# Bulk loads issued by ScalarE on a queue of their own, and bias loads two rounds later, in a two-layer attention and retention trunk

## The chip, the cores and the metric

The kernel runs on one core of a Trainium2 chip. The metric is the device time of one execution in microseconds (us); the median of several runs counts. TensorE (PE) multiplies matrices, VectorE (DVE), ScalarE (ACT) and GpSimd (POOL) do the element-wise work, and SyncE (SP) does no arithmetic: in the kernel before it issues every DMA. The DMAs move data on 16 DMA engines.

## The reference

A trunk of two layers works on 2048 tokens of width 1024. Each layer does

```python
hn = rms_norm(x, norm_gain)
proj = hn @ w_in                      # 1024 -> 8 sections of 512
aq, ak, av, ag, rq, rk, rv, rg = split(proj)
ya = chunked_rel_attention(aq, ak, av, rel_bias)   # 8 heads x 64, own chunk of 64 + 8 before, bias by distance
yr = chunkwise_retention(rq, rk, rv, cos, sin)     # 4 heads x 128, decay per head, rotary phases, RMS norm per head
y = concat([ya * silu(ag), yr * silu(rg)])
x = x + y @ w_out
```

and a last RMS norm with a gain follows. All is float32; the kernel makes each product of a high and a low float16 part, in three matmuls.

## The kernel before, in words

**Tiling and stages.** A layer `l` is worked through in four groups `s` (two attention heads and one retention head each), and a group in four blocks `n` of 512 tokens. For each block `dense_T` makes q, k and the rotary inputs (lines 736 and before) and `dense_V` makes v and the gates (line 755); the attention and the retention of a block run beside the dense products of the next one. After the four groups `wout` multiplies by `w_out` (line 1105) and adds the residual, 16 blocks of 128 tokens.

**Rounds.** All is laid out by hand in rounds: `run` steps the dense generator (8 matmuls of 128x512 a step), then the attention, and then pulls some steps of the background list `bg`. `later(k, fn)` runs `fn` k rounds on. A block is 24 rounds. What the rounds call is recorded on PE, ACT, DVE and POOL in exactly that order:

```python
ctx.enter_context(tc.manual_schedule(engines={E.PE, E.Activation, E.DVE, E.Pool}))
```

SP is in that list only for the start of the program (`sp_order`, up to the end of the first `dense_V`). After that the order of what SP issues is made by the scheduler of the layer below, which may put a load ahead of its place in the source; only the `toep` DMAs are held at their place (`keep_in_program_order`).

**The background work.** `prep_T` and `prep_V` bring a group's weights (tiles `stT`, `stV`, 512 KB each, through `load_sec`), take the sum of their squares on ACT (`sumsq`, line 312), derive a power-of-two scale, and split them on ACT (line 333) and DVE (line 336). `prep_Omax` goes through the eight column blocks of `w_out` (tiles `stO0m` in layer 0, `stO1m` in layer 1): it squares one, then loads the next. `prep_O` loads and splits `w_out` itself (`stO`). They share a pool of three buffers (`w4`).

**Attention.** For each unit (128 queries of one head): scores on PE (lines 803 and 804), bias and maximum on DVE (807), exponential and float16 rounding on ACT (810, 812), the low part on POOL (813), one DMA transpose `pT<-pq` issued by SP (815), and the product with v on PE (823 to 825), which comes two units later.

**Other loads.** `bias_scratch` writes two Toeplitz tables `toep` in DRAM for a group (line 567), and `bias_tiles` reads a `bias` tile from each (580) and scales it on ACT (584). `tab_load` brings the rotary tables `tabc` and `tabs` of a block (623, 624). `y_load` (935) and `x_load` (944) bring the blocks that `wout` works on, `Sections` brings the small mask `msk` (359), `norms_from_input` the tokens of the first layer. SP also issues what the chains wait for: `pT<-pq`, the rearranged `q<-qq` and `k<-kk`, `swp`, `kt<-rot`, the stores to `y_d` and `x_d`, and the transposes of `wout` and of the norms.

**Semaphores of the DMAs.** The layer below deals eight semaphores in turn to all DMAs, whichever engine issues them, and a DMA waits until the one that had its semaphore before has landed.

Of the kernel before, what the change touches and what calls it, by code (L numbers as in the profile page):

```python
# [18 lines left out]
P = 128  # L19
EPS = 1e-6  # L20
HALF_PI = 1.5707963267948966
RELW = 767
# [5 lines left out]
def hybrid_trunk(ctx: ExitStack, tc: tile.TileContext, x, pos, gain, gcol, w_in, w_out, rel, fgain,  # L28
# [8 lines left out]
    act, dve, pool, pe, sp = nc.scalar, nc.vector, nc.gpsimd, nc.tensor, nc.sync  # L37
# [30 lines left out]
    y_d = [dp.tile([P, D], F32, tag=f"y_d{t}", name=f"y_d{t}") for t in range(NT)]  # L68
    x_d = [dp.tile([P, D], F32, tag=f"x_d{t}", name=f"x_d{t}") for t in range(NT)]
    tab_d = [dp.tile([2, P, 512], F32, tag=f"tab{n}", name=f"tab{n}") for n in range(NS)]  # L70
# [218 lines left out]
    TSEC = (0, 1, 4, 5)  # L289
    VSEC = (2, 6, 3, 7)  # L290

    def load_sec(src, nm, halves=False):

        v = src.rearrange("(k p) c -> p k c", p=P)
        if not halves:
            st = w4.tile([P, KT, P], F32, tag="w4", name=f"st{nm}")
            sp.dma_start(st, v)
            return [(st, 0, KT)]
        h = KT // 2
        st = [b2.tile([P, 3 - i, 512], F16, tag=("rot2", "rot3")[i], name=f"st{nm}_{i}") for i in range(2)]  # L300
        st = [t_[:, 0:2].rearrange("p a c -> p (a c)").bitcast(F32).rearrange("p (k c) -> p k c", c=P) for t_ in st]
        for i in range(2):
            sp.dma_start(st[i], v[:, i * h:(i + 1) * h, :])
        return [(st[i], i * h, (i + 1) * h) for i in range(2)]

    keep = lambda i: i
# [10 lines left out]
    def lowp(m1, nm):  # L317
        mb = b2.tile([P, 1], BF16, tag="mb", name=f"mb{nm}", bufs=4)
        dve.tensor_copy(mb, m1)
        return mb  # L320
# [33 lines left out]
    class Sections:  # L354


        def __init__(self, l, s, g, halves=False):
            g.msk = b2.tile([P, P], F32, tag="msk", name=f"msk{l}_{s}")
            sp.dma_start(g.msk, dmask[:, s, :])
            g.rd, g.s = rdc[:, s:s + 1], s  # L360
            self.l, self.s, self.g, self.halves = l, s, g, halves
            self.nm = f"T{l}_{s}"
            self.sts, self.sq, self.iv, self.sv = [], [None] * 4, [None] * 4, [None] * 4
            g.h = b3.tile([P, 4, KT, P], F16, tag="wh", name=f"wh{self.nm}")
            g.l = b3.tile([P, 4, KT, P], F16, tag="wl", name=f"wl{self.nm}")
# [102 lines left out]
    def prep_V_next(l, g):  # L468

        nm = f"V{l}_0"  # L470
        src = [w_in[l, :, VSEC[j] * 512:VSEC[j] * 512 + P] for j in range(4)]
        sts = [load_sec(src[j], f"{nm}{j}", True) for j in range(2)]
        yield
        for j in (2, 3):
            st = b2.tile([P, KT, P], F32, tag="q", name=f"st{nm}{j}")
            sp.dma_start(st, src[j].rearrange("(k p) c -> p k c", p=P))
            sts.append([(st, 0, KT)])
        yield
        g.vh = b3.tile([P, KT, 512], F16, tag="wh", name=f"wh{nm}")
        g.vl = b3.tile([P, KT, 512], F16, tag="wl", name=f"wl{nm}")  # L480
        hi, lo = ([w_[:, :, j * P:(j + 1) * P] for j in range(4)] for w_ in (g.vh, g.vl))
        m = [lowp(sumsq(sts[j], f"{nm}{j}", hi[j]), f"{nm}{j}") for j in range(2)]
        yield
        m2, m3 = (sumsq(sts[j], f"{nm}{j}", hi[j]) for j in (2, 3))
        dve.tensor_tensor(m2, m2, m3, op=ALU.add)
        m.append(lowp(m2, f"{nm}2"))
        yield
        yield
        iv = [None] * 3
        for j in (2, 0, 1):  # L490
            sv, iv[j] = norm_scale(allsum(m[j], f"{nm}{j}"), f"{nm}{j}", gains[l].i)
            for i in ((2, 3) if j == 2 else (j,)):
                yield from convert(sts[i], hi[i], lo[i], sv)
        yield from V_units(l, 0, g, iv, nm)
        g.vdone = 4
# [37 lines left out]
    toep = {}  # L533
    NH = 4 * 2 * DEPTH
    rel_d = dp.tile([NH, RELW + 1], F32, tag="rel_d", name="rel_d")
# [27 lines left out]
    def bias_scratch(l, s):  # L563
        for hh in range(2):
            h = 2 * s + hh
            d = dp.tile([P * RELW], F32, tag=f"toep{h % 4}", name=f"toep{l}_{h}")
            i = sp.dma_start(d.rearrange("(p w) -> p w", w=RELW),
                             rel_d[l * 8 + h:l * 8 + h + 1, 1:RELW + 1].to_broadcast([P, RELW]))
            if (l, s) != (0, 0):
                tc.keep_in_program_order(i)  # L570
            toep[l, h] = d
        yield

    def bias_tiles(l, s, g):

        g.bias = []
        for hh in range(2):
            h = 2 * s + hh
            bt = b3.tile([P, 640], F32, tag="bias", name=f"bias{l}_{h}")
            sp.dma_start(bt, toep[l, h][127:127 + P * (RELW - 1)].rearrange("(p w) -> p w", w=RELW - 1)[:, 0:640])  # L580
            yield
            pool.memset(bt[64:128, 0:64], NEG)
            pool.memset(bt[0:64, 576:640], NEG)
            act.activation(bt, bt, AF.Copy, scale=g.ci[:, 0:1])
            g.bias.append(bt)
            yield
# [28 lines left out]
    def dense_T(l, s, n, g, st):  # L615
# [4 lines left out]
        def tab_load():  # L620
            while n not in tab_done:
                pull(1)
            sp.dma_start(st.tabc, tab_d[n][0])
            sp.dma_start(st.tabs, tab_d[n][1])

        first = (l, s, n) == (0, 0, 0)

# [299 lines left out]
    def y_load(l, t):  # L927
        u = St()
        u.nm = f"y{l}_{t}"
        u.t = t  # L930
        if t < 8:
            u.y = w4.tile([P, D], F32, tag="w4", name=f"yy{u.nm}")
        else:
            u.y = b2.tile([P, D], F32, tag="q", name=f"yy{u.nm}")
        sp.dma_start(u.y, y_d[t])
        return u

    def x_load(l, u):
        if l + 1 == DEPTH or u.t < 12:
            f = (hT[l, 0] if l + 1 == DEPTH else hT_of(l + 1, NS - 1))[u.t // 2 % 2].rearrange("p k c -> p (k c)").bitcast(F32)  # L940
            u.x = f[:, u.t % 2 * D:(u.t % 2 + 1) * D]
        else:
            u.x = w4.tile([P, D], F32, tag="w4", name=f"xx{u.nm}")
        sp.dma_start(u.x, x[u.t * P:(u.t + 1) * P, :] if l == 0 else x_d[u.t])

    def y_squares(l, u):
        u.m = b2.tile([P, 1], F32, tag="ym", name=f"ym{u.nm}")
# [218 lines left out]
    def norms_from_input(ts, spaces, rows, tab):  # L1166

        def load(k):
            u = us[k]
            u.x = spaces[k] if spaces else w4.tile([P, D], F32, tag="w4", name=f"xin{u.t}")  # L1170
            if not spaces:
                sp.dma_start(u.x, x[u.t * P:(u.t + 1) * P, :])

        def sq(k):
            u = us[k]
            u.h = [h_[:, :, u.t % 4 * P:(u.t % 4 + 1) * P] for h_ in hT_of(0, u.t // 4)]
            u.ss = squares(u.x.rearrange("p (k c) -> p k c", c=P), u.nm, u.h[0])

        def root(k):
            us[k].rs = rms_of(us[k].ss, gains[0].m, gains[0].e, us[k].nm)  # L1180

        def mul(k):
            u = us[k]
            dve.scalar_tensor_tensor(out=u.x, in0=u.x, scalar=u.rs[:, 0:1], in1=gains[0].b, op0=ALU.mult, op1=ALU.mult)

        def hi(k):
            us[k].rows = rows[k % 2]
            rows_hi(us[k].rows, us[k].x)

        def lo(k):  # L1190
            rows_lo(us[k].rows, us[k].x)

        def dma(k):
            transpose_rows(us[k].rows, *us[k].h)

        us = []
        for t in ts:
            u = St()
            u.t, u.nm = t, f"n0_{t}"
            us.append(u)  # L1200
        plan = {0: [lambda: load(0)]}
        add = lambda r, fn, k: plan.setdefault(r, []).append(lambda: fn(k))
        for k in range(4):
            if k:
                add(4 * k - 4, load, k)
            for i, fn in enumerate((sq, root, mul, hi, lo, dma)):
                add(3 + 4 * k + i, fn, k)
        for r in range(21):
            for fn in plan.get(r, ()):
                fn()  # L1210
            next(tab, None)
            yield
        for _ in tab:
            yield
# [156 lines left out]
    for l in range(DEPTH):  # L1371
        gO = [Grp(), Grp()]
        go = Grp()
        for s in range(NSW):
            g = grp(l, s)
            for n in range(NS):
                first = (l, s, n) == (0, 0, 0)
                if not first:
                    st = St()
                    states[l, s, n] = st  # L1380
                    dT = dense_T(l, s, n, g, st)
                else:
                    st = st0
                if n == 0 and not first:
                    bs, bt = bias_scratch(l, s), bias_tiles(l, s, g)
                    later(1, lambda bs=bs: next(bs))
                    for k in (4, 8, 17, 21):
                        later(k, lambda bt=bt: next(bt))
                if (l, s) == (0, 0) and 0 < n < NS - 1:
                    if n == 1:  # L1390
# [30 lines left out]
                run(dense_V(l, s, n, g, st), att, 24 if n == NS - 1 and s < NSW - 1 else 12)  # L1421
                if first:
                    sp_order.__exit__(None, None, None)
                if att[0] is not None:
                    drain(att[0])
                att = [attention(l, s, n, g, st, states.get((l, s, n - 1)))]
# [84 lines left out]
```

## Time and profile before

| | |
|---|---|
| time, median of 3 runs | 2089.06 us (2085.99 to 2094.31) |
| time of the profiled execution | 2090.77 us |
| span of the profiled execution, first to last instruction | 2089.0 us |
| PE busy | 2007.5 us, 96% |
| ACT, DVE, POOL busy | 1145.0, 1177.1, 676.1 us (55%, 56%, 32%) |
| DMA queue | one (hardware_dynamic), 311.12 MB, 65.2% of 16 engines' span |
| mean granted TensorE clock | 0.992 |

"Busy" counts the instructions of an engine that compute; issues of DMAs are shown on the queue of the issuing engine (SPq for SP's) and are not counted as busy. "DMA to landing" is the time from the start of an issue until the semaphore shows that all of it has arrived. A line number is that of the kernel before. In the waits, "A <- B" says that A's engine stood idle until B was done.

### The profile page before, as it was taken

How to read it: one execution, taken by the hardware profiler on the slowest of the kernel's cores; microseconds unless marked ns; L12 is line 12 of the kernel's file. 1: busy time of each engine (PE TensorE's matmuls, PEld its weight loads, DVE VectorE, ACT ScalarE, POOL GpSimd, SP SyncE). 2: the span in 40 equal slices, each digit the busy share in tenths (PEclk: the TensorE clock that was granted, in tenths of full speed). 3: DMA queues.
4: the chain of work that ended last, by engine and by line, in shares of the span. 5: the costliest groups of instructions: out<-in, count | busy, mean ns of one | idle time of the engine just before them, and what ended most of it. 6: DMA issues, size and time to landing. Idle time of an engine off the chain costs nothing.

```text
span 2089.0 us, 39378 instructions
## 1 busy us (share of the span) xinstructions
PE 2007.5 (96%) x14014; PEld 1051.1 (50%) x14014; DVE 1177.1 (56%) x3817; ACT 1145.0 (55%) x2530; POOL 676.1 (32%) x701
## 2 busy tenths in 40 slices
PE   6988999999999999999999999999999999999998
PEld 4444555555555555544444555555555555554543
DVE  6766556555545554576553545554555555447543
ACT  6556665556565654555444556554655565446432
POOL 0334343334333433330003433343243334333100
PEclk9999999999999999999999999999999999999999
DMA  8768674547575754799774547454655857548874
GB/s 231 171 148 172 146 160 106 117 113 155 116 183 117 155 143 102 157 226 271 187 195 101 120 102 152 111 123 105 148 121 121 175 144 167 116 102 190 211 197 125
DMA packets 645701, 313.63 MB, mean 150 GB/s; under 512 B 459232, under 2 KB 602080, under 8 KB 645504
## 3 DMA queue, kind: packets, MB, share of 16 engines
q1 hardware_dynamic: 645504, 311.12, 65.2%
q8 instruction: 109, 1.79, 0.4%
q14 instruction: 88, 0.72, 0.1%
HBM read 123.26 MB, written 41.98 MB: 79 GB/s over the span
## 4 chain that ended last, share of the span: by engine, by line
PE 49%; DMA 3%; ACT 2%; DVE 1%; issue 1%; SPq 0%; POOLq 0%; ACTq 0%; DVEq 0%
PE dT L736 15%; PE dV L755 14%; PE dO L1105 13%; PE r L857 2%; DMA pT<-pq 2%; PE S L804 1%; PE S L803 1%; PE o L823 1%; PE o L824 1%; PE o L825 1%; DMA toep<-rel_d 1%; ACT stO1m L312 0%; DMA yly<-hTl 0%; ACT sc L810 0%; DMA stO1m<-in_w_out_dram 0%
## 5 line engine op out<-in xcount | busy, mean ns | idle before, releaser
L813 POOL TENSOR_TENSOR pq<-sc,pq 128x640 f16<-128x640 f32 (+4 forms) x256 | 321.1, 1254 | 927.5 <-ACT pq L812 493.2
L810 ACT ACTIVATE sc<-sc,mq,cT 128x640 f32<-128x640 f32 (+4 forms) x256 | 218.5, 854 | 618.3 <-DVE rl L829 322.1
L755 PE MATMUL dV<-whV,hTh 128*128 128x512 f16 x1024 | 352.6, 380 | 4.3 <-DVE gt L773 4.3
L736 PE MATMUL dT<-hTh,whT 128*128 128x512 f16 x1008 | 350.3, 383 | 4.1 <-DMA hTh<-rows 2.1
L755 PE MATMUL dV<-whV,hTl 128*128 128x512 f16 x1024 | 352.3, 380 | 0.0
L755 PE MATMUL dV<-wlV,hTh 128*128 128x512 f16 x1024 | 352.1, 380 | 0.0
L736 PE MATMUL dT<-hTl,whT 128*128 128x512 f16 x1008 | 348.6, 381 | 0.0
L736 PE MATMUL dT<-hTh,wlT 128*128 128x512 f16 x1008 | 348.3, 381 | 0.0
L755 PEld LDWEIGHTS <-hTh 128*128 128x128 f16 x2048 | 196.3, 98 | 219.6 <-DVE gt L773 7.1
L736 PEld LDWEIGHTS <-whT 128*128 128x128 f16 x2016 | 193.1, 98 | 217.9 <-issue 13.0
L807 DVE CUSTOM_DVE_ANT_0 sc<-S,bias 128x640 f32<-128x640 f32 (+4 forms) x256 | 188.4, 736 | 143.1 <-PE S L804 141.8
L1105 PE MATMUL dO<-whO,yly 128*128 128x512 f16 x512 | 195.4, 382 | 3.7 <-DMA yly<-hTl 3.7
L1105 PE MATMUL dO<-whO,yhy 128*128 128x512 f16 x512 | 195.5, 382 | 0.0
L1105 PE MATMUL dO<-wlO,yhy 128*128 128x512 f16 x512 | 195.3, 382 | 0.0
L812 ACT ACTIVATE pq<-sc 128x640 f16<-128x640 f32 (+4 forms) x256 | 171.5, 670 | 8.1
L1105 PEld LDWEIGHTS <-yhy 128*128 128x128 f16 x1024 | 100.0, 98 | 116.3 <-issue 2.8
L755 PEld LDWEIGHTS <-hTl 128*128 128x128 f16 x1024 | 99.0, 98 | 110.0 <-issue 0.6
L736 PEld LDWEIGHTS <-wlT 128*128 128x128 f16 x1008 | 97.7, 98 | 111.8 <-issue 5.0
L823 PE MATMUL o<-v,pT 128*128 128x65 f16 x1120 | 130.0, 194 | 18.3 <-DMA pT<-pq 18.3
L803 PE MATMUL S<-k,q 128*128 128x128 f16 (+3 forms) x592 | 143.3, 268 | 0.0
L823 PEld LDWEIGHTS <-pT 128*128 128x128 f16 x1120 | 105.6, 97 | 55.4 <-DMA pT<-pq 27.0
L804 PE MATMUL S<-k,q 128*128 128x128 f16 (+3 forms) x592 | 130.6, 269 | 0.0
(352 smaller groups left out, 3421.0 us busy)
## 6 DMA issues: line engine op xcount, KB each, us to landing
q<-qq SPq DMA_DIRECT2D x128, 128.0 KB, 2.5
yyy<-y_d SPq DMA_DIRECT2D x32, 512.0 KB, 4.6
stT<-in_w_in_dram SPq DMA_DIRECT2D x27, 512.0 KB, 5.0
stV<-in_w_in_dram SPq DMA_DIRECT2D x26, 512.0 KB, 4.5
k<-kk SPq DMA_DIRECT2D x128, 64.0 KB, 2.0
swp<-rot SPq DMA_DIRECT2D x64, 128.0 KB, 2.7
tabc<-tab SPq DMA_DIRECT2D x32, 256.0 KB, 2.7
tabs<-tab SPq DMA_DIRECT2D x32, 256.0 KB, 3.2
```

What stands on the lines that cost most here:

```text
L736: pe.matmul(ps, w_[:, j, kt, :], h_[:, kt, :], start=(m == 0), stop=(m == 23))
L755: pe.matmul(ps, h_[:, kt, a * P:(a + 1) * P], w_[:, kt, :], start=(m == 0), stop=(m == 23))
L803: pe.matmul(o, st.q[:, hx, 0, cs], k_, start=True, stop=False)
L804: pe.matmul(o, st.q[:, hx, 1, cs], k_, start=False, stop=True)
L807: dve.tensor_tensor_reduce(out=v, in0=S[:, 0:w], in1=g.bias[hx][:, 640 - w:640], scale=1.0, scalar=-3.0e38, op0=ALU.add, op1=ALU.max, accu ...
L810: act.activation(v, v, AF.Exp, bias=m[:, 0:1], scale=g.c[:, 0:1])
L812: act.activation(pq[:, 0:w], v, AF.Copy)
L813: pool.tensor_tensor(pq[:, w:2 * w], v, pq[:, 0:w], op=ALU.subtract)
L823: pe.matmul(o[:, 0:65], u.p[:, b, :], v_[:, 0:65], start=(b == 0), stop=False)
L824: pe.matmul(o[:, 0:64], u.p[:, b, :], v_[:, 65:129], start=False, stop=False)
L857: pe.matmul(out_, w_, m_, start=(i == 0), stop=(i + 1 == len(pairs)))
L1105: pe.matmul(ps, h_[:, kt, :], w_[:, kt, :], start=(m == 0), stop=(m == 23))
```

## The change

A function `bring` issues a load on SP up to the end of the first `dense_V` and on ACT from there on (`nc.scalar.dma_start`, a hardware queue of its own). The loads of weights, masks, rotary tables, Toeplitz tables and bias tiles, `wout`'s blocks and the first layer's tokens go through it. ACT's order is the recorded one, so each of these loads stands on ACT at its place in the source. The four steps of a group's bias tiles are called in rounds 6, 10, 19 and 22 instead of 4, 8, 17 and 21. No load is added or taken away, and no instruction of an engine's arithmetic.

```diff
+    bulk = {"e": sp}
+
+    def bring(dst, src):
+
+        return bulk["e"].dma_start(dst, src)
+
     def load_sec(src, nm, halves=False):
...
-            sp.dma_start(st, v)
+            bring(st, v)
...
-            sp.dma_start(st[i], v[:, i * h:(i + 1) * h, :])
+            bring(st[i], v[:, i * h:(i + 1) * h, :])
...
-            sp.dma_start(g.msk, dmask[:, s, :])
+            bring(g.msk, dmask[:, s, :])
...
-            sp.dma_start(st, src[j].rearrange("(k p) c -> p k c", p=P))
+            bring(st, src[j].rearrange("(k p) c -> p k c", p=P))
...
-            i = sp.dma_start(d.rearrange("(p w) -> p w", w=RELW),
-                             rel_d[l * 8 + h:l * 8 + h + 1, 1:RELW + 1].to_broadcast([P, RELW]))
-            if (l, s) != (0, 0):
-                tc.keep_in_program_order(i)
+            bring(d.rearrange("(p w) -> p w", w=RELW),
+                  rel_d[l * 8 + h:l * 8 + h + 1, 1:RELW + 1].to_broadcast([P, RELW]))
...
-            sp.dma_start(bt, toep[l, h][127:127 + P * (RELW - 1)].rearrange("(p w) -> p w", w=RELW - 1)[:, 0:640])
+            bring(bt, toep[l, h][127:127 + P * (RELW - 1)].rearrange("(p w) -> p w", w=RELW - 1)[:, 0:640])
...
-            sp.dma_start(st.tabc, tab_d[n][0])
-            sp.dma_start(st.tabs, tab_d[n][1])
+            bring(st.tabc, tab_d[n][0])
+            bring(st.tabs, tab_d[n][1])
...
-        sp.dma_start(u.y, y_d[t])
+        bring(u.y, y_d[t])
...
-        sp.dma_start(u.x, x[u.t * P:(u.t + 1) * P, :] if l == 0 else x_d[u.t])
+        bring(u.x, x[u.t * P:(u.t + 1) * P, :] if l == 0 else x_d[u.t])
...
-                sp.dma_start(u.x, x[u.t * P:(u.t + 1) * P, :])
+                bring(u.x, x[u.t * P:(u.t + 1) * P, :])
...
-                    for k in (4, 8, 17, 21):
+                    for k in (6, 10, 19, 22):
...
                 if first:
                     sp_order.__exit__(None, None, None)
+                    bulk["e"] = act
```

## The prediction

> **What bounds the kernel now.** I read the busy shares first, then what PE waited for, then what SP waited for.
>
> ```profile
> PE 2007.5 (96%) x14014; PEld 1051.1 (50%) x14014; DVE 1177.1 (56%) x3817; ACT 1145.0 (55%) x2530; POOL 676.1 (32%) x701
> PE o L823 <- DMA pT<-pq: 18.3, 13, 3.1
> PE r L857 <- DVE dT L865: 11.5, 14, 2.3
> SPq L580 <- DMA toep<-rel_d: 28.8, 7, 4.5
> ```
>
> PE computes 2007.5 of 2089.0 us, so at most 81.5 us can be won by taking waits away. A row of waits gives the total, the count and the longest. The only large wait that SP's order can cause is the first: 18.3 us for the transposed probabilities, which SP issues. ACT is idle for 2089.0 - 1145.0 = 944 us, but every engine runs its instructions in order, so it matters more who stands behind a waiting one.
>
> What I compare the orders of the two kernels for is where a load stands. PE's and DVE's orders are the same in both. SP loses 259 loads, which ACT gets: 2237 rows of ACT become 2496. Before, the scheduler put a load far ahead of its reader on SP. Afterwards it stands at its place in the source, and there the next ACT instruction, or one of the next eight, reads it.
>
> **A, the bias tiles (gain).** SP at the start of group 1 of layer 1, and what PE had of it:
>
> ```profile
> 1270.08 1.33 SPq L815 DMA_TRANSPOSE pT<-pq  x1
> 1272.82 1.22 SPq L567 DMA_DIRECT2D toep<-rel_d  x2
> 1278.48 0.34 SPq L580 DMA_DIRECT2D bias<-toep  x1
> 1279.40 3.97 SPq L815 DMA_TRANSPOSE pT<-pq  x1
> 1286.15 0.20 PE L823 MATMUL o<-v,pT 128*128 128x65 f16 x1 [2.21 <-DMA pT<-pq]
> core 0: us, PE busy (x) PEld busy (x) DVE busy (x) ACT busy (x) POOL busy (x), PEclk, DMA share, GB/s
> 1287.00:1291.00 4.00, 4.00 (x19) 1.74 (x18) 1.64 (x8) 2.36 (x8) 0.64 (x1) 0.57 0.75 167
> 1495.00:1499.00 4.00, 3.45 (x29) 2.36 (x30) 1.26 (x5) 0.17 (x1) 0.00 (x0) 0.57 0.89 171
> 1707.00:1711.00 4.00, 4.00 (x27) 2.18 (x24) 1.64 (x8) 1.33 (x2) 0.00 (x0) 0.57 0.67 158
> ```
>
> From the end of the `toep` issue (1274.04) SP stood 4.44 us until `bias` could be issued at 1278.48, and the next transpose took 3.97 instead of 1.33 us to issue: together 7.1 us late, of which PE saw 2.21. So PE had about 4.9 us in hand; I use that cover again below. Behind that wait the granted clock is 0.57 for 4 us, which loses 4 x 0.43 = 1.7 us. The same stretch of low clock stands in three groups of layer 1. With the loads off SP that wait goes: 3 x (2.2 + 1.7) = 12 us less. Bounds: 0, if ACT's wait for `toep` stops PE just as long (the two rounds more make that less likely), and 18.3 + 3 x 1.7 = 23 us less, if every wait for `pT` goes. I take 12, since the other ten waits show no such cause.
>
> **B, the maximum over `w_out` (loss).** `prep_Omax` squares a block and then loads the next. Before, SP had issued the first three far ahead:
>
> ```profile
> L297 SPq DMA_DIRECT2D stO0m<-in_w_out_dram x8: 380/460/623, 547.1 to 612.0; - x8
> L312 ACT ACTIVATE stO0m<-stO0m x8: 1039/1040/1057, 598.3 to 617.4; 128x1024 f32<-128x1024 f32 x8
> DMA to landing us min/median/max: 4.3/5.1/5.8
> DMA to landing us min/median/max: 4.1/5.0/5.9
> 596.75 0.92 ACT L810 ACTIVATE sc<-sc,mq,cT 128x640 f32<-128x640 f32 x1 [3.82 <-DVE mq L809]
> 597.71 0.74 ACT L812 ACTIVATE pq<-sc 128x640 f16<-128x640 f32 x1
> 598.35 1.04 ACT L312 ACTIVATE stO0m<-stO0m 128x1024 f32<-128x1024 f32 x1
> 617.38 1.06 ACT L312 ACTIVATE stO0m<-stO0m 128x1024 f32<-128x1024 f32 x1
> 547.00:598.00 51.00, 51.00 (x369) 26.97 (x368) 27.61 (x104) 28.49 (x69) 19.27 (x19) 1.00 0.61 127
> 598.00:620.00 22.00, 20.69 (x156) 10.79 (x155) 11.44 (x44) 18.73 (x46) 9.04 (x8) 1.00 0.92 231
> 1614.00:1636.00 22.00, 20.59 (x153) 10.65 (x151) 11.37 (x44) 18.61 (x46) 8.96 (x8) 1.00 0.91 230
> PE r L857 <- ACT dT L861: 1.3, 1, 1.3
> ```
>
> (The second landing row is that of `stO1m`, layer 1; the last row is PE's waits in 596 to 640.) The first load was issued 51 us ahead of its square, and the eight squares took 19.0 us from first to last. In the changed order ACT has `pq`, load, square, load, three instructions, square, load, five instructions, square and so on: each load is issued only when the square ahead of it has gone, and ACT stands at the next square until it has landed. The set then takes eight landings in a row. Of the median 5.1 and the shortest 4.1 us I take 4.7, as the loads no longer queue behind SP's others. The last square begins at 598.35 + 8 x 4.7 = 635.95 instead of 617.38: 18.6 us later. Does it reach PE? In 598 to 620 ACT is busy 18.73 of 22 us and PE already stands 1.3 us there for ACT, so PE has nothing in hand by then; ACT empties PE's accumulators (lines 763 to 766) between the squares. Both layers: +37 us. Low: 8 x 4.1 = 32.8, +13.8 each, 28. High: a load that is issued only when the square has ended, 8 landings of 5.1 and 7 squares of 1.04 = 48.1, +29 each, 58.
>
> In 598 to 620 the DMA engines are busy to 0.92. The Trainium skill, "DMA: Bandwidth & Descriptors", section "Issuing engines are not separate DMA queues", says that DMAs started by different engines run on the same 16 engines and that a second issuer saves only the time of issuing. By it a landing on ACT's queue keeps 5.1 us, and B would be 2 x (8 x 5.1 - 19.0) = 44 instead of 37 us; no run of the kernel before shows a second queue.
>
> **C, the first loads of the other helpers (loss).**
>
> ```profile
> stT<-in_w_in_dram SPq DMA_DIRECT2D x27, 512.0 KB, 5.0
> stV<-in_w_in_dram SPq DMA_DIRECT2D x26, 512.0 KB, 4.5
> stO<-in_w_out_dram SPq DMA_DIRECT2D x16, 512.0 KB, 5.0
> yyy<-y_d SPq DMA_DIRECT2D x32, 512.0 KB, 4.6
> 269.45 0.53 SPq L297 DMA_DIRECT2D stT<-in_w_in_dram  x1
> 316.56 0.26 ACT L920 ACTIVATE r<-r 128x128 f32<-128x128 f32 x1
> 316.84 1.04 ACT L312 ACTIVATE whT<-stT 128x1024 f16<-128x1024 f32 x1
> 1785.53 0.42 SPq L297 DMA_DIRECT2D stO<-in_w_out_dram  x1
> 1890.30 1.13 ACT L333 ACTIVATE whO<-stO,o_s 128x1024 f16<-128x1024 f32 x1
> ```
>
> A weight block lay 47 us (`stT`) or 105 us (`stO`) ahead of its reader. Now a set of `stT` is `pq`, three issues (`msk`, two blocks), line 920, the square: ACT stands for one landing. The later blocks of a set are issued while the one before is worked on, rounds ahead, and cost nothing; if that cover went, each would cost what the first does. Holds of the first loads: six sets of `stT`, six of `stV`, four in the two sets of `stO` for each layer, one at each start of `wout`. What a hold costs PE is landing plus issues (about 0.4 us each) less the cover of 4.9: `stT` 5.0 + 1.2 - 4.9 = 1.3, `stV` 4.5 + 0.9 - 4.9 = 0.5, `wout` 0.6. For `stO` I take half the cover, as PE already waits in 14 places for `dT` beside it (11.5 us): 5.0 + 0.4 - 2.4 = 3.0. Sum 8 + 3 + 12 + 1 = 24 us. Bounds: 0 when all are covered; with half the cover everywhere 6 x 3.8 + 6 x 3.0 + 12 + 2 x 3 = 59.
>
> **D, the issuing itself.** 259 x 0.46 = 119 us of ACT's time, in 944 us of idle time, spread over all rounds: +2, bounds 0 and 10 (a twelfth of it on PE). **E, other waits of the issues on ACT:** for one of the eight dealt semaphores, and `wout`'s blocks where a layer passes into the next: +2, 0 to 10. **F, clock:** in B ACT sets the pace whatever the clock is, so only the end of each set and some holds of C pay 1.7 us: 3 x 1.7 = +5, 0 to 8.
>
> **Sum.** -12 + 37 + 24 + 2 + 2 + 5 = +58 us. The profiled execution took 2090.8 us (span 2089.0) and lies 1.7 above the median of 2089.1. 2089.1 + 58 = **2147 us**.
>
> **The rivals.**
>
> *Faster: the loads go out ahead of ACT's standing instructions.* If ACT issues a load while earlier instructions still wait, then the eight-instruction distance is time. It decides from about 5 us of lead: ACT waited 3.82 us for the maximum just ahead of the first square of B, nearly a landing. Then B and C vanish and the gain of A stays, at most all 18.3 us of the waits for `pT`: 2089.1 - 18.3 = 2071 us. For it: ACT is idle 45% of the time. Against it: in B each load stands behind a square, which waits for the load ahead, so the lead cannot grow there. The Trainium skill, "Advanced Engine Details and Errata", section "Sequencer Loop", says that instructions can be read and queued while one that came earlier is still held; the rows of before show no DMA on ACT to try that on. Chance 0.10.
>
> *No change: the holds are covered.* If PE has the 4.9 us in hand in B too, and C costs nothing, 2 x (13.8 - 4.9) = 18 of B and 12 of gain remain: 2095 us. The 1.3 us wait in B speaks against. Chance 0.07.
>
> *Much slower: two issuers hold each other up.* SP's transpose took 3.97 instead of 1.33 us to issue just behind other DMAs. If an issue of ACT is lengthened by those 2.6 us, the 16 loads of B and 18 of C pay it in full: 34 x 2.6 = 88, 2236 us. Chance 0.08.
>
> **How the numbers follow.** The forecast's case has 0.75. Its bounds: at the low end -12 + 28 + 0 = 16 or, with A at its largest, 5: 2094. At the high end B +21 and C +35 more than taken: 2203. I leave out the faster and the much slower rival (0.18) and take in the covered one: 2093 to 2205. A measurement of this kernel can tell about 0.5% (10 us) from no change. Faster is the first rival, 0.10; within 0.5% the second, 0.07; the rest, 0.83, is slower.
>
> **What would show it.** Right: in the profile after, ACT stands 3 to 5 us ahead of each square of `stO0m` and `stO1m`, and their eight squares last 33 to 40 us instead of 19; PE's waits gain rows that end on ACT, or on the `stO` and `stT` loads; SP's row for `toep` is gone, and with it PE's three waits of over 2 us for `pT`. A is wrong if these waits stay; B if the squares still take about 20 us, or take longer while PE does not stop; C if ACT's waits for first loads appear and PE has none beside them. The whole is wrong if loads are issued well ahead of their readers on ACT, or if the median is under 2093.

## The result

The changed kernel takes 2176.12 us (median of 4 runs, 2175.28 to 2185.18) against 2087.97 us: a ratio of 1.0427, 95% interval 1.0391 to 1.0462. The forecast was 2147; the loss is 88 us where 58 were expected. The profiled execution has a span of 2174.7 us, 85.7 more than before.

The busy shares of the profile after:

```profile
PE 2027.9 (93%) x14014; PEld 1056.7 (49%) x14014; DVE 1173.1 (54%) x3817; ACT 1149.4 (53%) x2530; POOL 673.9 (31%) x701
q1 hardware_dynamic: 530128, 202.52, 45.4%
q10 hardware_dynamic: 115376, 108.60, 18.0%
```

PE computes the same 14014 matmuls and is busy 20.4 us longer (a lower clock, 0.978 instead of 0.992), so 65.3 of the 85.7 us are idle PE. A second hardware queue (the last row) now carries 108.60 MB. What PE waited for (total us, times, longest):

```profile
PE r L861 <- ACT dT L865: 28.1, 7, 7.4
PE r L861 <- DVE dT L869: 26.6, 18, 3.1
PE o L827 <- DMA pT<-pq: 16.3, 14, 2.6
PE dO L1109 <- DMA yly<-rly: 7.4, 2, 3.9
PE dO L1109 <- DMA yly<-hTl: 7.0, 2, 4.8
PE dO L1109 <- DMA yhy<-rhy: 4.3, 1, 4.3
```

The first row was 3.3 us before:

```profile
PE r L857 <- ACT dT L861: 3.3, 3, 1.4
```

The last three rows after belong to `wout`, where the forecast had next to nothing. And what ACT waited for, of the loads it now issues itself:

```profile
ACT whT L318 <- DMA stT<-in_w_in_dram: 20.7, 6, 5.3
ACT whO L339 <- DMA stO<-in_w_out_dram: 20.4, 8, 4.0
ACT stO1m L318 <- DMA stO1m<-in_w_out_dram: 17.0, 6, 5.6
ACT stO0m L318 <- DMA stO0m<-in_w_out_dram: 15.9, 7, 4.6
ACT L814 <- DMA tab<-xa: 9.1, 1, 9.1
```

**A ledger by stretches.** PE's order is the same in all these kernels, so the n-th matmul of one trace can be set beside the n-th of another. By how many us each stretch became longer than in the kernel before (its bounds are times of before; in brackets the part that is idle PE, the rest is clock):

| stretch | what lies in it | after |
|---|---|---|
| 75 to 150 | first attention beside the tables | +7.0 (7.1) |
| 150 to 250 | first `stT` set on ACT | +6.2 (2.6) |
| 600 to 650 | Omax, layer 0 | +16.9 (12.4) |
| 950 to 1090 | first `wout`, with layer 1's first weights | +25.7 (19.4) |
| 1260 to 1320, 1480 to 1520, 1690 to 1730 | starts of groups 1, 2, 3 of layer 1 | -2.0, -2.9, -1.0 |
| 1600 to 1650 | Omax, layer 1 | +19.8 (14.0) |
| 1880 to 1930 | `stO`, layer 1 | +4.2 (4.2) |
| 1930 to 2080 | second `wout` | +0.9 (0.7) |
| all others together | | +10.9 |

One trace of each kernel stands behind such a ledger, and a stretch does not repeat exactly: in the seven kernels that have the first `stT` set on ACT, 150 to 250 reads +3.8 to +9.0, and 650 to 950 reads +4.5 to +15.8. Differences of a few us in these two are therefore no finding.

**Omax.** The tile `stO0m` and ACT's timeline in the changed kernel:

```profile
L296 ACTq DMA_DIRECT2D stO0m<-in_w_out_dram x8: 374/374/417, 613.0 to 644.4; - x8
L318 ACT ACTIVATE stO0m<-stO0m x8: 1040/1056/1057, 618.4 to 648.8; 128x1024 f32<-128x1024 f32 x8
DMA to landing us min/median/max: 4.3/4.3/5.3
```

```profile
613.00 0.74 ACT L816 ACTIVATE pq<-sc 128x640 f16<-128x640 f32 x1
613.01 0.42 ACTq L296 DMA_DIRECT2D stO0m<-in_w_out_dram  x1
618.36 1.06 ACT L318 ACTIVATE stO0m<-stO0m 128x1024 f32<-128x1024 f32 x1 [4.62 <-DMA stO0m<-in_w_out_dram]
618.36 0.39 ACTq L296 DMA_DIRECT2D stO0m<-in_w_out_dram  x1
622.71 1.06 ACT L318 ACTIVATE stO0m<-stO0m 128x1024 f32<-128x1024 f32 x1 [2.12 <-DMA stO0m<-in_w_out_dram]
```

The load leaves with the start of the instruction ahead of it (`pq` at 613.00, the square at 618.36), and then ACT stands until it has landed. From the first load to the last square pass 648.8 - 613.0 = 35.8 us.

**The start.** ACT, and PE just behind, about 100 us:

```profile
88.12 0.57 ACT L656 ACTIVATE kk<-dT 128x512 f16<-128x512 f32 x1
96.22 0.34 ACTq L296 DMA_DIRECT2D tabc<-tab  x1
97.42 0.33 ACTq L296 DMA_DIRECT2D tabs<-tab  x1
97.83 1.28 ACT L814 ACT_TABLE_LOAD   x1 [9.14 <-DMA tab<-xa]
```

```profile
100.79 0.39 PE L861 MATMUL r<-rv,dT 128*128 128x128 f16 x2 [7.40 <-ACT dT L865]
```

The load of the rotary table (`tabc<-tab`) waits for the store that writes this table (`tab<-xa`). The exponential (line 814, with the `ACT_TABLE_LOAD` ahead of it) and `dT` stand behind it on ACT, and PE stands 7.4 us.

**The first `wout`.** The same 480 matmuls of it in the kernel before and in the changed one (columns as in the first row), then the transposes of two neighbouring blocks on SP in each, before first:

```profile
core 0: us, PE busy (x) PEld busy (x) DVE busy (x) ACT busy (x) POOL busy (x), PEclk, DMA share, GB/s
965.50:1065.20 99.70, 99.61 (x480) 47.77 (x481) 57.29 (x121) 43.31 (x72) 4.93 (x9) 0.98 0.83 212
```

```profile
1003.80:1127.50 123.70, 105.58 (x480) 49.52 (x481) 61.64 (x131) 46.87 (x77) 4.95 (x9) 0.90 0.89 198
```

```profile
1015.04 1.58 SPq L236 DMA_TRANSPOSE yly<-rly  x1
1023.51 1.32 SPq L236 DMA_TRANSPOSE yly<-rly  x1
```

```profile
1062.15 4.20 SPq L236 DMA_TRANSPOSE yly<-rly  x1
1072.15 3.60 SPq L236 DMA_TRANSPOSE yly<-rly  x1
```

The DMA engines are fuller (0.89) and move less in a second (198 GB/s). The two transposes, which stay on SP, take 3.6 to 4.2 instead of 1.3 to 1.6 us to issue. They are among the longest: the median of these issues (`yly`) in the first `wout` is 1.8 instead of 1.6 us. What grew throughout is the time to landing. PE stood there seven times, 22.9 us in all, in five blocks, each time for a transpose (before, once for 3.7 us). Measured from PE's start on the block ahead, the low part's transposes of these five blocks were issued from 3.1 us earlier to 1.0 us later than before, but took 7.0 to 11.3 us to land, where they took 3.3 to 5.6. So they were not late because ACT had been held; they landed late.

### The profile page after: what moved, and what is told of

It reads as the page before. It is cut to its first block, busy times and chain, and to the rows that moved or that the text cites. A ratio compares the mean times of both kernels' runs of the same rounds, so it can differ in the third digit from the quotient of the medians.

```text
span 2174.7 us, 39229 instructions
## 1 busy us (share of the span) xinstructions
PE 2027.9 (93%) x14014; PEld 1056.7 (49%) x14014; DVE 1173.1 (54%) x3817; ACT 1149.4 (53%) x2530; POOL 673.9 (31%) x701
## 3 DMA queue, kind: packets, MB, share of 16 engines
q10 hardware_dynamic: 115376, 108.60, 18.0%
## 5 line engine op out<-in xcount | busy, mean ns | idle before, releaser
L807 PE MATMUL S<-k,q 128*128 128x128 f16 (+3 forms) x592 | 142.7, 267 | 2.9 <-DVE mq L811 2.9
L828 PE MATMUL o<-v,pT 128*128 128x64 f16 x1120 | 131.3, 196 | 0.0
```

The costliest lines, as they stand in the source:

```text
L807: pe.matmul(o, st.q[:, hx, 0, cs], k_, start=True, stop=False)
L828: pe.matmul(o[:, 0:64], u.p[:, b, :], v_[:, 65:129], start=False, stop=False)
```

## The experiments

The theory is that the loss comes where a load stands just ahead of its reader on ACT, and is paid at these places. The rival is that each issue on ACT, or the second queue itself, costs its share everywhere. In the experiments `bring` takes the kind of a load and leaves some kinds on SP, whose order the scheduler makes as before:

```diff
-    def bring(dst, src):
-        return bulk["e"].dma_start(dst, src)
+    def bring(dst, src, kind):
+        e = bulk["e"] if kind in ON_ACT else sp
+        return e.dma_start(dst, src)
```

The kinds are `w` (`load_sec`), `omax`, `next` (layer 1's first weights), `msk`, `toep`, `bias`, `tab`, `yx` (`wout`'s blocks), `xin` (first tokens). A ratio is to the kernel before, run on the same chip.

**1. Omax back on SP**

```diff
+    ON_ACT = ("bias", "msk", "next", "tab", "toep", "w", "xin", "yx")
```

> Only the 16 loads of prep_Omax (stO0m, stO1m) go back to SP; the other 243 stay on ACT. Theory (ACT stands at the reader of a load that lies just ahead of it): the 37 us that matching PE instructions fall back across the two sets are gone, about 2139 us, and the eight squares take about 19 us again. Rival (each issue on ACT costs its time, and two issuers slow each other): 16 of 259 issues of a loss of 88 us, 5 us, about 2171 us.

Ratio 1.0272 (1.0253 to 1.0291), 32 us less than the changed kernel by the ratios. The two Omax stretches went from +16.9 and +19.8 to +1.4 and +0.3; the first `wout` stayed at +22.5. The theory holds here; a share by the count of issues would have been 5 us.

**2. Layer 1's first weights back on SP**

```diff
+    ON_ACT = ("bias", "msk", "omax", "tab", "toep", "w", "xin", "yx")
```

> Only the weight loads of layer 1's first group (half blocks stT, stV, and two whole stV blocks, brought during the first wout) go back to SP. Theory: these issues wait on ACT for buffers and semaphores, and hold the row conversions that wout's transposes wait for; without them the 26 us lost in the first wout are gone, about 2150 us. Rival (wout loses through its yyy and x blocks on ACT, which stay there): the first wout still loses about 25 us, no change at 2176 us.

Ratio 1.0404 (1.0382 to 1.0427): its interval overlaps that of the changed kernel. In its profile the first `wout` still lost 16.9 of 25.7 us. My expectation failed: these weights are the smaller part. The 8.8 us that it won there do not show clearly in the total, as stretches that the edit does not touch were longer in this trace (150 to 250, 250 to 600 and 650 to 950 by 2.8 to 3.5 us each).

**3 to 5. The gain: toep and bias**

The third kernel has only these on ACT, the fourth only the two rounds, the fifth the queue with the first tile's steps as early as before:

```diff
 # third
+    ON_ACT = ("bias", "toep")
+                    for k in (6, 10, 19, 22):
 # fourth: toep held at its place, as before
+    ON_ACT = ()
+                    for k in (6, 10, 19, 22):
 # fifth
+    ON_ACT = ("bias", "toep")
+                    for k in (4, 8, 19, 22):
```

> Only the toep and bias loads go to ACT, with the bias steps two rounds on; all else stays on SP in its scheduled order. Theory: PE's waits for pT at the starts of the groups of layer 1 go, 9 to 12 us less, 2076 to 2079 us. Rival (ACT stands for the bias tile instead and PE with it, or other loads on SP take the place): 2088 us or more.

> All loads on SP as before, toep still held at its place; only the bias steps come in rounds 6, 10, 19, 22 instead of 4, 8, 17, 21. Theory that the gain is owed to the queue: SP still stands at toep, 2088 us. Rival that the two rounds alone give toep the time to land: SP's 28.8 us wait for toep is gone and the kernel is 9 to 12 us faster, 2076 to 2079 us.

> Only toep and bias on ACT, with the first tile's steps in rounds 4 and 8 as before and the second tile's in 19 and 22. Theory (the queue alone brings the gain, PE has cover for a hold on ACT): the group starts of layer 1 gain 9 us as with rounds 6 and 10, ratio 0.997. Rival (the two rounds are needed: ACT stands for toep in SP's place): under 4 us gained there, ratio 1.000 or above.

Ratios: third 0.9973 (0.9962 to 0.9983), fourth 1.0010 (0.9999 to 1.0020), fifth 0.9956 (0.9941 to 0.9970). At the starts of groups 1, 2 and 3 of layer 1 the third gained 2.9 + 3.5 + 2.9 = 9.3 us, the fourth lost 0.5, the fifth gained 3.5 + 4.4 + 3.3 = 11.2. In the fourth SP still stood for `toep`, since the scheduler kept `bias` right behind it, and PE's waits for `pT` were not less than before:

```profile
SPq L299 <- DMA toep<-rel_d: 28.2, 7, 4.6
PE o L832 <- DMA pT<-pq: 20.0, 13, 3.3
```

So the gain is owed to taking these loads off SP's order and not to the two rounds. The fifth has the lowest ratio here, 9 us under the kernel before; its interval overlaps that of the third.

**6. The same gain on SP?**

```diff
 # the fourth, and:
+            i = bring(bt, toep[l, h][...], "bias")
+            if (l, s) != (0, 0):
+                tc.keep_in_program_order(i)
```

> All loads on SP as before, the bias steps in rounds 6, 10, 19, 22, and the bias load held at its place in the source like toep, so that it stands seven issues behind toep and not right behind it. Theory (what was lost is SP's standing for toep, so the distance brings the gain and no second queue is needed): SP's 28.8 us wait for toep goes, ratio 0.997. Rival (other loads of SP or the single queue still delay the transposes): 1.000 or above.

Ratio 0.9980 (0.9969 to 0.9991), group starts 1.8 + 2.7 + 1.8 = 6.3 us less. SP's row for `toep` is gone. PE's waits for `pT` in 1255 to 1760 us were 7.6 us in 3 times before; here there are four short ones. Their row, then SP at the start of group 1:

```profile
PE o L834 <- DMA pT<-pq: 2.5, 4, 0.9
```

```profile
1279.35 1.22 SPq L299 DMA_DIRECT2D toep<-rel_d  x2
1282.90 3.89 SPq L826 DMA_TRANSPOSE pT<-pq  x1
```

In these traces two thirds of the third kernel's gain (6.3 of 9.3 us) need no second queue; the intervals of the two ratios overlap. The transpose behind `toep` still takes 3.89 us to issue (3.97 before), so that part was not due to SP's standing. In the third kernel, with `toep` on ACT, the transposes there took 1.3 and 2.0 us.

**7. Omax on ACT, but issued ahead**

```diff
-        st = load_sec(w_out[l, :, 0:P], f"{nm}m0")
+        sts = [load_sec(w_out[l, :, j * P:(j + 1) * P], ...) for j in range(3)]
+        yield
...
-            if j + 1 < KT:
-                st = load_sec(w_out[l, :, (j + 1) * P:(j + 2) * P], f"{nm}m{j + 1}")
+            if j + 3 < KT:
+                sts.append(load_sec(w_out[l, :, (j + 3) * P:(j + 4) * P], ...))
...
-        for _ in range(4):
+        for _ in range(3):
```

> All loads on ACT as in the changed kernel, but prep_Omax issues three loads ahead of its first square and then each load three squares ahead of its own (three buffers as before). Theory of holds (distance decides, not the engine): as when the Omax loads were on SP, 32 us less than the changed kernel, ratio to before 1.027, no wait of ACT for stO0m, squares in about 20 us. Rival (the second queue or the issue on ACT itself costs it): unchanged, ratio 1.043.

Ratio 1.0359 (1.0343 to 1.0374): 14 us less than the changed kernel, not 32. The tile `stO0m` (with ACT's standing for it) and ACT's timeline:

```profile
L321 ACT ACTIVATE stO0m<-stO0m x8: 1040/1043/1056, 622.2 to 643.3; 128x1024 f32<-128x1024 f32 x8
  DMA stO0m<-in_w_out_dram: 0.9, 1
DMA to landing us min/median/max: 5.1/6.1/10.9
```

```profile
623.43 0.38 ACTq L299 DMA_DIRECT2D stO0m<-in_w_out_dram  x1
623.85 0.28 ACT L771 ACTIVATE v<-dV 128x128 f16<-128x128 f32 x1 [0.45 <-ACT stO0m L321]
```

ACT's standing is gone (0.9 for 15.9 us), the squares take 21 us, and the two stretches fell from +16.9 and +19.8 to +4.9 and +6.5. So it is the distance, not the engine, that makes most of Omax's loss. What is left may come from two things that the rows show: three loads together take longer to land (median 6.1 instead of 4.3 us), and a load into the buffer just squared waits for that square's end, which leaves ACT idle 0.45 us where the next instruction is ready. The two stretches won 25.3 us, the whole kernel 14: the stretch from 650 to 950 became 11.3 us longer than in the changed kernel, 4.6 of it up to 760, and why is open.

**8. All weights back on SP**

```diff
+    ON_ACT = ("bias", "tab", "toep", "xin", "yx")
```

> All weight loads and masks (load_sec, the Omax set, layer 1's first group, msk) back on SP; toep, bias, tables, wout's blocks and the first tokens stay on ACT. By the theory of holds, stretch by stretch: the 6 us at 150 to 250 us of before (stT directly ahead of its square), 37 us of the two Omax sets and the 4 us at 1880 to 1930 (stO) go; the 7 us at 75 to 150 us stay, since there ACT waits with a table load for the stores of the table; the first wout keeps about 17 us; the group starts gain 9. About 15 us slower than before, ratio 1.007. Rival (loss goes by the count of issues on ACT, 160 of 259): 50 us, ratio 1.024.

Ratio 1.0127 (1.0104 to 1.0149). The places of the theory went as expected: 150 to 250 from +6.2 to -1.5, Omax to -0.3 and +1.6, 1880 to 1930 to +0.2; the start kept +8.4. From 900 to 1125, where `wout`'s blocks are on ACT, it lost 19.3 us in all where 17 were expected, and the group starts gained 5.1 instead of 9. With the start this makes most of what it was slower than expected; the rest is spread.

**9. wout's blocks on SP, ahead and late**

```diff
 # ahead, as the scheduler puts them
+    ON_ACT = ("bias", "msk", "next", "omax", "tab", "toep", "w", "xin")
 # late: the same, and each held at its place in the source
+        tc.keep_in_program_order(bring(u.y, y_d[t], "yx"))
+        tc.keep_in_program_order(bring(u.x, ..., "yx"))
```

> The changed kernel with wout's blocks (y and x loads) alone back on SP. With layer 1's weights alone back on SP the first wout still lost 17 of 26 us. Theory (the y and x loads go out too late behind ACT's waits, and the transposes that read them late): 17 us or more of the first wout go, ratio about 1.035, nothing else changes. Rival (the loss needs either set: whichever stays on ACT holds it): first wout loses over 15 us again, ratio 1.041.

> As the changed kernel, with wout's y and x blocks on SP but held at their place in the source, so that they are issued about as late as on ACT, on the queue that the transposes use. Theory of lateness (a late transfer falls among the transposes and is read at once, whoever issues it): the first wout loses 20 us or more again, ratio 1.04. Rival (a second queue that takes turns with the queue of the transposes lengthens them, 3.6 to 7.9 us for the low part's): the first wout loses about 8 us as when SP issued these blocks ahead, ratio 1.036 or less.

Ratios 1.0395 (1.0376 to 1.0414) and 1.0392 (1.0369 to 1.0414); the stretch of the first `wout` +7.8 and +9.3 instead of +25.7. Held, the blocks of the first `wout` were squared as they landed, 0.0 to 0.1 us later for 14 of 16, so they were at least as late as on ACT, and still it lost only 9.3. So lateness is not what costs most there. The landing of the low part's transposes (tile `yly`) in the first `wout`: before, changed, on SP ahead, on SP held:

```profile
DMA to landing us min/median/max: 2.7/3.6/5.7
```

```profile
DMA to landing us min/median/max: 3.1/6.7/11.3
```

```profile
DMA to landing us min/median/max: 2.7/3.7/7.1
```

```profile
DMA to landing us min/median/max: 3.1/5.2/9.0
```

They are lengthened by late blocks on the same queue (5.2 instead of 3.7 us), and more when the blocks come through the second queue (6.7); PE pays 1.5 us for the first step and 16.4 for the second. Over the 480 matmuls shown above, the DMA engines moved 222 GB/s at a share of 0.91 with the blocks held on SP, and 198 at 0.89 with them on ACT. In the second `wout` the same blocks on ACT cost 0.9 us, with no other weights moved, at a share of 0.84 of the DMA engines, and the median landing of `yly` is 4.1 us there in both kernels.

The ratios do not follow: the first `wout` won 17.9 and 16.4 us, the whole kernel only about 7. So the held kernel's ratio lies near the 1.04 of the theory of lateness, but the stretch, which that theory was about, speaks against it. What was lost elsewhere is spread over many stretches (650 to 950 became 5.4 and 2.0 us longer than in the changed kernel) and was not taken apart.

**10. The tables of layer 0's first group**

```diff
+    ON_ACT = ("bias", "msk", "tab", "toep", "w", "xin")
-            bring(st.tabc, tab_d[n][0], "tab")
+            bring(st.tabc, tab_d[n][0], "tab0" if (l, s) == (0, 0) else "tab")
```

> As the changed kernel, with the Omax loads, layer 1's first weights and wout's blocks on SP, and the tables of layer 0's first group as well; the rest stays on ACT. Theory (ACT stood 9 us with a table load for the store of the table, the first tokens' loads cost nothing): the 7 us at 75 to 150 us of before fall to under 3, both Omax sets and the first wout lose under 3 us each, and 10 us remain of stT and stO: ratio 1.003 to 1.008. Rival (the tokens' loads hold ACT there): 7 us stay at 75 to 150, ratio over 1.008.

Ratio 1.0129 (1.0104 to 1.0153). The start fell from +7.0 to +0.3 and the first `wout` to -4.4: both causes are confirmed where they lie. The -4.4 is partly moved to the stretches beside it; from 900 to 1125 it is +0.5, where the changed kernel has +24.7. But the whole is slower than expected: 650 to 950 lost 15.2 us (4.5 in the changed kernel), in waits for `pT`. That was not taken apart.

**11. Toep, bias and the later tables on ACT**

```diff
+    ON_ACT = ("bias", "tab", "toep")
+            bring(st.tabc, tab_d[n][0], "tab0" if (l, s) == (0, 0) else "tab")
```

> As the kernel with only toep and bias on ACT (ratio 0.997), with the rotary tables on ACT as well from group 1 of layer 0 on. SP stood 55 us in 27 waits of the table loads for the rotation. Theory: those waits hold transposes on SP, so up to 5 us more are gained, ratio 0.995. Rival: on ACT the tables are issued behind waits of ACT and the rotation reads them late: 0.997 or above.

Ratio 1.0026 (1.0015 to 1.0038). The rival: the tables cost more on ACT than SP's 55 us of waits for them did. It lost 3.8 us in 650 to 760 and 5.5 where layer 1 begins (1090 to 1125).

## Why the prediction was right in direction and too small

**What bounds the kernel: right.** PE computes the same matmuls, and 65.3 of the 85.7 us are waits. Most of them lie where ACT stands for a load (26.4 in Omax, 7.1 at the start); in the first `wout` (19.4) they end on SP's transposes.

**A, forecast -12:** the three waits of over 2 us went, as said, but the whole change kept only 2.0 + 2.9 + 1.0 = 5.9 (2.7 to 5.9 in the seven kernels with the other weights on ACT). With nothing else on ACT it is 9.3 to 11.2, so the step was sized well and eaten up in part by other loads on ACT. Of the 7.1 us late, the transpose's long issue (2.6) was not SP's standing (experiment 6). The two rounds were not needed (experiments 3 to 5).

**B, forecast +37:** 16.9 + 19.8 = 36.7. The landing was 4.3 us where I took 4.7; first load to last square 35.8 where 37.6 was worked out. Experiments 1 and 7 show place and mechanism. On the page "DMA: Bandwidth & Descriptors" of the Trainium skill, section "Issuing engines are not separate DMA queues", a second issuer saves only issuing time, and by it B would have been 44. Here the loads of Omax landed in 4.3 instead of 5.1 us, and B came out by 4.3 to 4.7. That is no proof against the page: the loads came one at a time, 4.3 was the shortest landing before too, and three at a time on ACT took 6.1 (experiment 7). That all DMAs interleave on the same 16 engines agrees with the `yly` rows of experiment 9. That the issuer makes no other difference does not: the same blocks, as late, left +25.7 us in the first `wout` through ACT's queue and +9.3 through SP's.

**C, D and F, forecast 24 + 2 + 5 = 31:** what the ledger leaves beside A, B and E is 85.7 + 5.9 - 36.7 - 32.7 = 22.2 us. So the sum was high by 9. The two places that experiment 8 tried were right, the first `stT` set and `stO` of layer 1, and make 6.2 + 4.2 = 10.4 of it; the rest was not taken apart. For F, PE is busy 20.4 us longer, of which 36.7 - 26.4 = 10.3 lie in Omax, where B already held them, and 6.3 in the first `wout`; the group starts give back 4.5, which A holds. That leaves 8.3 us for the other places, against 5 and at the upper bound of 8.

**E, forecast +2, bounds 0 to 10:** this is the step that failed: 7.0 + 25.7 = 32.7 us. I had named waits for semaphores and `wout`'s blocks where a layer passes into the next; the weights of layer 1's first group stood in no term, as C counts six of the seven sets that ACT brings. Two things stood in its place. A load on ACT can wait for its *source* (the table's store, 9.1 us), not only for its landing; the lead that I counted was that to the reader. And in the first `wout` the bulk loads on a second queue lengthen the transposes that PE waits for. That is near the third rival, two issuers that hold each other up, but it is SP's transposes that suffer and not ACT's issues, and in one place. Blocks and weights moved there share the loss. From 900 to 1125 the changed kernel lost 24.7 us; with only the weights back on SP 17.3 remain, with only the blocks 9.0, with both 0.5. In the kernel with only the blocks back, PE's waits there end on three transposes. Measured as above, these were issued no later than before, and they landed in 6.8 to 9.1 instead of 3.9 to 5.6 us. Whether the weights do this by the queue or by coming later is open, as no run holds them late on SP.

That the measured time lies in the stated range is in part luck: E went 31 us over, and what kept the sum in was that the upper ends of B and C were not needed.

**The rivals.** In the rows shown, loads do leave before the instruction ahead of them has ended, but only one instruction ahead, and those behind still stand: the faster case would have needed more. By the Trainium skill, "Advanced Engine Details and Errata", section "Sequencer Loop", an engine's instructions are pushed into a queue and wait there for their semaphores, and others can be read and queued while microcode executes. The trace agrees for one instruction, 613.01 beside 613.00. That holds are covered fell with PE's row for ACT's `dT`, 28.1 us.

## What to carry to other kernels

A load given to a computing engine stands in that engine's order: before moving it, look at how far ahead of its reader, and behind which writer of its source, it will stand; if the distance is under a landing (4.3 to 5.1 us here), everything behind it pays. Move only those loads that made the old queue stand (here `toep` and `bias`, 0.4% faster in the best form), and look first whether holding them some issues further back on the old queue does most of it. Where transposes that TensorE waits for share busy DMA engines (0.83 here before the change), look at their landing before putting bulk transfers on a second queue beside them. And read a ledger to its end: in experiments 2, 7 and 9 a kernel won 9 to 25 us at the place that was changed, and only 5 to 14 in the whole.

## What was not expected of the hardware

In the first `wout`, with 512 KB loads on a second queue, the low part's transposes on the first landed in 6.7 instead of 3.6 us (median of 16), and with the blocks among these loads as late on the first queue in 5.2. PE lost 25.7 and 9.3 us there. In the second `wout`, with the DMA engines' share at 0.84, they landed in 4.1 us with and without the second queue, and 0.9 us was lost. A DMA issue on ACT cost no time beside a running instruction (issued at 618.36 with the square that began at 618.36), but 0.45 us of idle ACT where it had to wait for the end of the instruction just ahead.
